# An MLP whose quarters end in a plain pair of tiles, and two first tiles that follow x together

## The chip, the cores and the metric

The kernel runs on one core of one Trainium2 chip. The core has five engines with instruction streams of their own: TensorE (PE) multiplies, VectorE (DVE) and ScalarE (ACT) do arithmetic on tiles, GpSimd (POOL) and SyncE (SP) here mostly issue DMA transfers. The engines wait for one another by semaphores. The metric is the time of one execution on the device, in microseconds; less is better.

## The reference

Two layers over 512 tokens of 1024 features. Layer 0 mixes tokens with an mLSTM (projections of x into q, k, v, an output gate and eight gate columns; a causal convolution of four taps and SiLU on q and k), layer 1 with causal pooling. Each layer then attends to 256 memory tokens and applies an MLP. After every part x becomes LayerNorm(alpha x + part(x)). The two parts that the change touches are:

```python
proj = x @ w_in                     # q, k, v, output gate, 8 gate columns
qk = silu(causal_dwconv(proj[..., :nqk], conv_w))
gates = proj[..., nqk + nv + D_MODEL:] + gate_b
...
def sq_relu_mlp(x, w1, b1, w2, b2):  # w1: 1024 x 4096, w2: 4096 x 1024
    return square(relu(x @ w1 + b1)) @ w2 + b2
```

## The kernel before

Every float32 operand of a product is split into a high part and a low part that TensorE takes at its faster float32 rate, and each product is three matmuls (`mm3`, L198 to L200): high by high, high by low, low by high. So a weight tile of 128 x 1024 comes by DMA from SP (`raw`), is cast by ScalarE (`wh`, L161) and subtracted by VectorE (`wl`, L162). `unit` does that; its first tiles take their raw space from a pool `xs`, later ones from `raw_p`.

**Front.** After a few warm-up matmuls x arrives transposed in eight K tiles (`xr`, 256 KB each), each split like the weights. The feature tile 0 of q and k (`qk0`) has weights of its own, `u0`, that come in two halves between the tiles of x. The gate weights `wgt` come ahead of K tile 2; `pg`, 16 matmuls, is the product for the gates. The scheduler of the framework puts matmuls in an order by when their operands are due, so pg's stand between qk0's while x arrives. Then come qk4 (24 matmuls), v in four token tiles (v00 to v03) and the other q and k tiles. Work that need not be done at once is deferred: `defer` and `chain` give it a time in microseconds of matmul work, and `tick`, called by each `mm3`, issues it when that time is up. The gate arithmetic (`gates`, ending in Abs, Exp and Ln on ScalarE and a scan on VectorE), its rows, its transposed `columns` and the score tiles are such work.

**MLP.** The 4096 hidden features go in four quarters q; `up_down(q)` does 0, 1 and 2. The *up phase* makes eight feature tiles of 128 in pairs m = 0, 2, 4, 6. A plain pair is two `feat_tile`s of 24 matmuls of 512 columns each, with Relu and Square by `ev` (a tile `r`, then `s`). A pair whose number stands in `STRASSEN_UP[q]` goes through `up_pair`: seven products of 12 matmuls of 256 columns into banks `ua`, `ub`, `uc`, with sums and differences of weights made by VectorE; then copies, Relu and Square into the pair's two rows of `s`. In quarter 1 the pairs 1, 2, 3 go that way and pair 0, the first, is plain; in quarter 2 all four; in quarter 0 none (its first four tiles go together).

The *down phase* is Strassen's scheme again, on blocks of 512 x 512, each block 24 matmuls of 512 columns: `u` (a11 by b11), `f` (q1 by t1), `m2` (a12 by b21), and u, u, f, u once more. In the names of tiles `h` and `l` are the high and the low part, and the two digits ahead of them are layer and quarter: q101h is the high part of q1 in layer 0, quarter 1. `q1` is the block a21 - a22 of the quarter's activations, so it needs all eight feature tiles. `t1` is a sum of two weight blocks that a DMA makes: `onto_w` (L968) lets GpSimd issue a transfer that adds the second block onto the raw tile of b11. It can go only when b11's own cast (ScalarE) and subtract (VectorE) in `weight_split` (L787, L788) have read that tile. Each block is two tiles, so two transfers. The activations are split by `split` (L778, L779).

Per engine the instructions run in program order, which the framework's scheduler settles when the kernel is built.

Of the kernel before, what the change touches and what calls it, by code (L numbers as in the profile page):

```python
# [9 lines left out]
F32 = mybir.dt.float32  # L10
# [5 lines left out]
P = 128  # L16
D = 1024
# [16 lines left out]
SUM = sum(SEG)  # L34
WU = 1024
LN_T = 7.2
STRASSEN_UP = ((), (1, 2, 3), (0, 1, 2, 3))


def f32(ap):  # L40
# [4 lines left out]
def trunk(ctx: ExitStack, tc: tile.TileContext, a: dict, out: bass.AP):  # L45
# [45 lines left out]
    def ld(dst, src):  # L91
        nc.sync.dma_start(dst, src)
# [58 lines left out]
    def unit(src):  # L151
        n = n_units[0]
        n_units[0] += 1
        if n < 5:
            r = xs_p.tile([P, D], F32, tag="xs", name=f"raw{n}")
        else:
            r = raw_p.tile([P, WU], F32, tag="raw", name=f"raw{n}")
        ld(r, src)
        h = wh_p.tile([P, WU], F32R, tag="wh", name=f"wh{n}")
        l = wl_p.tile([P, WU], F32R, tag="wl", name=f"wl{n}")  # L160
        A.copy(h, r)  # L161
        V.tensor_tensor(l, r, f32(h), ALU.subtract)  # L162
        return h, l

    def m_unit(src):
        h, l = unit(src)
        return h.rearrange("p (k m) -> p k m", m=P), l.rearrange("p (k m) -> p k m", m=P)
# [9 lines left out]
    def defer(us, fn):  # L177

        later.append([us, fn])

    def chain(us, step, fns):
        for n, fn in enumerate(fns):
            defer(us + step * n, fn)
# [13 lines left out]
    def mm3(out_, l, r, start, stop, skip=False):  # L197
        T.matmul(out_, l[0], r[0], start=start, stop=False, skip_group_check=skip)  # L198
        T.matmul(out_, l[0], r[1], start=False, stop=False, skip_group_check=skip)  # L199
        T.matmul(out_, l[1], r[0], start=False, stop=stop, skip_group_check=skip)  # L200
        if later:
            tick(3 * max(r[0].shape[-1], 128) / 2400)
# [13 lines left out]
    def hf_cols(hf):  # L216
        return slice(hf * 512, (hf + 1) * 512)
# [79 lines left out]
        for i in range(n):  # L297
            evac(i, ps[i])

    def feat_tile(name, src, x, pool_, tag, cols=slice(0, S), u=None):  # L300
        u = u or m_unit(src)
        ps = pool_.tile([P, 512], F32, tag=tag, name=name)[:, : cols.stop - cols.start]
        for k in range(KC):
            mm3(ps, (u[0][:, k], u[1][:, k]), x.k(k, cols), start=k == 0, stop=k == KC - 1)
        return ps
# [21 lines left out]
        return t  # L327

    x0 = Act("x0")
    u0 = [xs_p.tile([P, D], F32, tag="xs", name="u0r")]  # L330
    u0 += [z.tile([P, WU], F32R, tag=t, name=f"u0{t}") for z, t in ((wh_p, "wh"), (wl_p, "wl"))]

    def u0_part(z):
        r, h, l = (w[:, hf_cols(z)] for w in u0)
        ld(r, a["w_qk"][0][:, hf_cols(z)])
        A.copy(h, r)
        V.tensor_tensor(l, r, f32(h), ALU.subtract)

    wgt = None
    for q in range(4):  # L340
        if q == 1:
            wgt = gate_weights()
        r = vkv(f"xr{q}", F32)[:, : 2 * S].rearrange("p (z t) -> p z t", z=2)
        for z in range(2):
            k = 2 * q + z
            ld(r[:, z], a["xT"][:, k])
            h, l = x0.k(k)
            A.copy(h, r[:, z])
            V.tensor_tensor(l, r[:, z], f32(h), ALU.subtract)
            if k % 4 == 0:  # L350
                u0_part(k // 4)
    u0 = [w.rearrange("p (k m) -> p k m", m=P) for w in u0[1:]]

    pg = tmp_p.tile([P, 512], F32, tag="tmp", name="pg")
    for k in range(KC):
# [9 lines left out]
        return qk.k(4 * (h // 2) + h % 2), qk.k(4 * (h // 2) + 2 + h % 2)  # L365

    def conv(c):
        ps = feat_tile(f"qk{c}", a["w_qk"][c], x0, aux_p, "aux", u=u0 if c == 0 else None)
        ac = t2(f"ac{c}")
        A.activation(ac, ps, AF.Copy, scale=convw[:, c, 3:4])  # L370
        for j in range(1, 4):
            V.scalar_tensor_tensor(ac[:, j:], ps[:, : S - j], convw[:, c, 3 - j : 4 - j], ac[:, j:], ALU.mult, ALU.add)
        f = t2(f"f{c}")
        A.activation(f, ac, AF.Silu)
        h, l = qk_k(c % H)[c // H]
        if c < H:
            A.activation(h, f, AF.Copy, scale=DK ** -0.5)
            V.scalar_tensor_tensor(l, f, DK ** -0.5, f32(h), ALU.mult, ALU.subtract)
        else:
            A.copy(h, f)  # L380
            V.tensor_tensor(l, f, f32(h), ALU.subtract)
# [84 lines left out]
        A.activation(emcol.rearrange("p a b -> p (a b)"), pc[:, 16:32], AF.Exp, scale=-1.0)  # L466

    chain(5, 3.5, [gates] + [lambda s=s: gate_rows(s) for s in range(NT)])
    defer(21, columns)
    for j, c in enumerate((5, 2, 6, 3, 7, None, None, None)):  # L470
        hf, t = j // 4, j % 4
        if j == 4:
            w_v = h_units(a["w_v"][hf])
        ps = token_proj(f"v{hf}{t}", x0, w_v, t)
        for q in range(2):
            h = 2 * hf + q
            split_psum((vh[h][:, t, :256], vl[h][:, t, :256]), ps[:, q * 256 : (q + 1) * 256])
        if c is not None:
            conv(c)
        if j in (0, 2, 4):  # L480
            chain((18, 13, 10)[j // 2], 2, scores(j // 2))

    normg = const_tile("normg", [P, KC])
    b1 = const_tile("b1", [P, DEPTH, DFF // P])
# [169 lines left out]
    for i in range(DEPTH):  # L654
# [147 lines left out]
        def block(r, c):  # L802

            return xm.half(c, slice(256 * r, 256 * r + 256))

        def x_sums():
# [42 lines left out]

            chain(3, 5, [start, q3, q1, q2, q4, end])  # L850

        def up_pair(q, m, n, s):


            src = [a["w1"][i, 8 * q + m + z] for z in range(2)]
            h2 = slice(0, 512), slice(512, 1024)
            u1, u2 = [raw_p.tile([P, WU], F32, tag="raw", name=f"up{n}{m + z}") for z in range(2)]
            ld(u1, src[0])
            ld(u2, src[1])
            ta, tb = [scoped["rawd"].tile([P, WU], F32, tag="rawd", name=f"ut{n}{m}{z}") for z in "ab"]  # L860

            def hl(name, r):
                h, l = [p.tile([P, WU], F32R, tag=t, name=f"{name}{n}{m}{t}")[:, : r.shape[1]] for p, t in ((wh_p, "wh"), (wl_p, "wl"))]
                A.copy(h, r)
                V.tensor_tensor(l, r, f32(h), ALU.subtract)
                return [tuple(z[:, c].rearrange("p (k m) -> p k m", m=P) for z in (h, l)) for c in h2[: r.shape[1] // 512]]

            b11, b21 = hl("ub", u1)
            V.tensor_tensor(ta[:, h2[0]], u1[:, h2[0]], u2[:, h2[0]], ALU.add)
            V.tensor_tensor(tb[:, h2[0]], ta[:, h2[0]], u2[:, h2[1]], ALU.add)  # L870
            V.tensor_tensor(tb[:, h2[1]], tb[:, h2[0]], u1[:, h2[1]], ALU.add)
            t2_, t4 = hl("utb", tb)
            V.tensor_tensor(ta[:, h2[1]], u2[:, h2[0]], u2[:, h2[1]], ALU.add)
            t1, t3 = hl("uta", ta)
            (b22,) = hl("ud", u2[:, h2[1]])

            pa = acc_p.tile([P, 512], F32, tag="acc", name=f"ua{n}{m}")[:, :256]
            pb = acc_p.tile([P, 512], F32, tag="acc", name=f"ub{n}{m}")[:, :256]
            pc = aux_p.tile([P, 512], F32, tag="aux", name=f"uc{n}{m}")[:, :256]
            z1, z2 = s[:, m % 4], s[:, m % 4 + 1]  # L880
            lo, hi = slice(0, 256), slice(256, 512)

            def prod(ps, w, x_, start):
                for k in range(4):
                    mm3(ps, (w[0][:, k], w[1][:, k]), (x_[0][:, k], x_[1][:, k]), start=start and k == 0, stop=k == 3, skip=not start)

            prod(pa, b11, block(0, 0), True)
            A.copy(z1[:, lo], pa)
            prod(pc, b21, block(0, 1), True)
            V.tensor_tensor(z1[:, lo], z1[:, lo], pc, ALU.add)  # L890
            prod(pa, t2_, xq["q2"], False)
            A.activation(z2[:, lo], pa, AF.Copy, scale=-1.0)
            prod(pb, t1, xq["q1"], True)
            A.copy(z2[:, hi], pb)
            prod(pa, t3, xq["q3"], False)
            V.tensor_tensor(z2[:, hi], z2[:, hi], pa, ALU.subtract)
            prod(pb, b22, xq["q4"], False)
            V.tensor_tensor(z2[:, lo], z2[:, lo], pb, ALU.add)  # L898
            prod(pa, t4, block(1, 1), False)
            A.copy(z1[:, hi], pa)  # L900
            for c, z in enumerate((z1, z2)):
                A.activation(z, z, AF.Relu, bias=b1[:, i, 8 * q + m + c : 8 * q + m + c + 1], scale=1.0)  # L902
                A.activation(z, z, AF.Square)

        def up_down(q, n):

# [38 lines left out]
            for m in range(first, KC, 2):  # L945
                if m // 2 in STRASSEN_UP[q]:
                    up_pair(q, m, n, s[m // 4])
                else:
                    for z in range(2):
                        ev(m + z, feat_tile(f"h{n}{m + z}", a["w1"][i, 8 * q + m + z], xm, aux_p, "aux"))  # L950
                if m == 2:
                    first_blocks()

            def onto(row, hf, op=ALU.add):
# [150 lines left out]
```

## Time and profile before

| what | us |
|---|---|
| median of 3 runs | 1243.29 |
| lowest, highest | 1242.1, 1243.35 |
| the profiled execution, its own time | 1241.42 |
| its span in the trace | 1239.7 |
| PE busy in it | 1191.8 |
| DVE busy | 857.7 |
| ACT busy | 617.9 |
| POOL busy | 62.1 |

A span counts from the first to the last instruction; what the execution takes beyond it lies around it. Matmuls overlap in the pipeline, so a single row's duration of 0.39 us is not its price: the distance between the starts of two rows is. The mean granted TensorE clock of this execution was 0.981 of full.

### The profile page before, as it was taken

Reading aid. Unit: us, or ns where it says so; the run is one execution under the profiler, and the core shown is the slowest. Engines: PE = TensorE matmul, PEld = TensorE weight load, DVE = VectorE, ACT = ScalarE, POOL = GpSimd, SP = SyncE. Lnnn points to the kernel's source line nnn. Section 1 sums busy time; section 2 is a strip of 40 time slices with the busy share of each in tenths; the row PEclk is TensorE's granted clock in tenths of the full one; section 3 lists DMA queues with packets and bytes.
Section 4 is the critical chain, followed back from the end, with each engine's and each line's share of the span. In section 5 each row is a group of like instructions: output and inputs, shape, how many; then the busy total and the mean of one; then the engine's idle time right before and its main releaser. Section 6 shows DMA issues by size and latency. Waiting matters only on the chain.

```text
span 1239.7 us, 16808 instructions
## 1 busy us (share of the span) xinstructions
PE 1191.8 (96%) x6609; PEld 1035.7 (84%) x6609; DVE 857.7 (69%) x1191; ACT 617.9 (50%) x924; POOL 62.1 (5%) x99
## 2 busy tenths in 40 slices
PE   9999999999999999799799999999999979979997
PEld 7888898898889789689688889988988968968886
DVE  6673575575567996597585599866889659758336
ACT  6585864135324646446446443652464554644430
POOL 0221000000000100100100000000010010010000
PEclk9999999999999999899899999999999989989999
DMA  8253258433255535835745455626453482583411
GB/s 277 77 143 108 86 189 294 146 103 102 82 156 154 102 85 168 172 68 175 165 114 194 127 185 195 192 86 186 139 117 79 158 175 65 181 177 85 119 52 68
DMA packets 50976, 171.85 MB, mean 139 GB/s; under 512 B 6336, under 2 KB 6604, under 8 KB 50896
## 3 DMA queue, kind: packets, MB, share of 16 engines
q1 hardware_dynamic: 42960, 142.96, 35.8%
q0 software_dynamic: 7936, 27.81, 12.5%
q8 instruction: 52, 0.85, 0.3%
q14 instruction: 28, 0.23, 0.1%
HBM read 164.43 MB, written 6.31 MB: 138 GB/s over the span
## 4 chain that ended last, share of the span: by engine, by line
PE 79%; DVE 9%; DMA 5%; ACT 4%; issue 2%; SPq 0%; DVEq 0%; ACTq 0%
PE h L198 5%; PE h L199 5%; PE h L200 5%; PE m L199 3%; PE m L198 3%; PE m L200 3%; DMA b<-in_w 3%; PE u L198 2%; PE u L199 2%; PE u L200 2%; PE ao L198 2%; PE ao L200 2%; PE ao L199 2%; PE q L198 2%; PE q L199 2%; PE q L200 2%
## 5 line engine op out<-in xcount | busy, mean ns | idle before, releaser
L162 DVE TENSOR_TENSOR wl<-raw,wh 128x1024 fp32r<-128x1024 f32 x147 | 179.1, 1220 | 145.9 <-ACT wh L161 143.9
L161 ACT CAST wh<-raw 128x1024 fp32r<-128x1024 f32 x147 | 153.7, 1049 | 226.3 <-PE h L199 52.4
L968 POOL DMA_DIRECT2D b<-in_w x36 | 31.7, 882 | 282.4 <-DVE b1100l L788 62.7
L968 POOL DMA_DIRECT2D t<-in_w x12 | 11.5, 996 | 680.0 <-DMA t<-in_w 451.2
L249 ACT ACTIVATE rs<-mv,eps_t 128x1 f32<-128x1 f32 x24 | 7.1, 295 | 53.2 <-DVE mv L247 53.2
L198 PE MATMUL h<-xm10h,wh 128*128 128x512 f32 (+1 forms) x88 | 31.0, 352 | 0.0
L198 PE MATMUL h<-xm00h,wh 128*128 128x512 f32 (+1 forms) x88 | 31.0, 352 | 0.0
L198 PE MATMUL h<-xm01h,wh 128*128 128x512 f32 (+1 forms) x88 | 31.0, 352 | 0.0
L198 PE MATMUL h<-xm11h,wh 128*128 128x512 f32 (+1 forms) x88 | 31.0, 352 | 0.0
L199 PE MATMUL h<-xm00l,wh 128*128 128x512 f32 (+1 forms) x88 | 30.9, 352 | 0.0
L199 PE MATMUL h<-xm10l,wh 128*128 128x512 f32 (+1 forms) x88 | 30.9, 351 | 0.0
L200 PE MATMUL h<-xm00h,wl 128*128 128x512 f32 (+1 forms) x88 | 30.8, 350 | 0.0
L200 PE MATMUL h<-xm01h,wl 128*128 128x512 f32 (+1 forms) x88 | 30.8, 350 | 0.0
L200 PE MATMUL h<-xm10h,wl 128*128 128x512 f32 (+1 forms) x88 | 30.8, 350 | 0.0
L200 PE MATMUL h<-xm11h,wl 128*128 128x512 f32 (+1 forms) x88 | 30.8, 350 | 0.0
L199 PE MATMUL h<-xm01l,wh 128*128 128x512 f32 (+1 forms) x88 | 30.8, 350 | 0.0
L199 PE MATMUL h<-xm11l,wh 128*128 128x512 f32 (+1 forms) x88 | 30.8, 350 | 0.0
L677 ACT ACTIVATE pr<-s,nm 128x256 f32<-128x256 f32 x32 | 14.9, 471 | 10.4 <-DVE nm L672 7.6
L902 ACT ACTIVATE s<-s,b 128x512 f32<-128x512 f32 x28 | 18.9, 718 | 2.0 <-DVE s L898 2.0
L199 PEld LDWEIGHTS h<-xm10l,wh 128*128 128x128 f32 x88 | 16.7, 189 | 2.3
L199 PEld LDWEIGHTS h<-xm00l,wh 128*128 128x128 f32 x88 | 16.7, 189 | 2.2
L198 PEld LDWEIGHTS h<-xm00h,wh 128*128 128x128 f32 x88 | 16.7, 189 | 2.2
(1696 smaller groups left out, 4259.3 us busy)
## 6 DMA issues: line engine op xcount, KB each, us to landing
raw<-in_w SPq DMA_DIRECT2D x60, 512.0 KB, 3.8
b<-in_w SPq DMA_DIRECT2D x36, 512.0 KB, 4.5
b<-in_w POOLq DMA_DIRECT2D x36, 512.0 KB, 5.7
up<-in_w SPq DMA_DIRECT2D x28, 512.0 KB, 3.7
raw<-in_w_q SPq DMA_DIRECT2D x24, 512.0 KB, 4.1
raw<-in_w_ao SPq DMA_DIRECT2D x16, 512.0 KB, 3.7
t<-in_w SPq DMA_DIRECT2D x12, 512.0 KB, 3.8
t<-in_w POOLq DMA_DIRECT2D x12, 512.0 KB, 9.8
```

The source lines that it names most:

```text
L161: A.copy(h, r)
L162: V.tensor_tensor(l, r, f32(h), ALU.subtract)
L198: T.matmul(out_, l[0], r[0], start=start, stop=False, skip_group_check=skip)
L199: T.matmul(out_, l[0], r[1], start=False, stop=False, skip_group_check=skip)
L200: T.matmul(out_, l[1], r[0], start=False, stop=stop, skip_group_check=skip)
L249: A.activation(rs, mv[:, 1:2], AF.Sqrt, bias=eps_t, scale=1.0)
L677: A.activation(pr[:, ms], ps[:, ms], AF.Exp, bias=nm[:, t_ : t_ + 1], scale=1.0, accum_out=sm[:, t_ : t_ + 1])
L902: A.activation(z, z, AF.Relu, bias=b1[:, i, 8 * q + m + c : 8 * q + m + c + 1], scale=1.0)
L968: G.dma_start(z[w], a["w2"][i, q, hf, j + w], accum_op=ALU.add)
```

## The change

Three things. In the MLP `STRASSEN_UP` names the pairs 0, 1, 2 in both quarters 1 and 2: in quarter 1 the plain pair moves from the first place to the last, in quarter 2 the fourth pair becomes plain. The seventh product of a Strassen pair, with the copies, Relu and Square of both its rows, is kept in `open_pairs` and issued by `last_product` behind the first product of the next pair, and for the last pair behind the first plain tile. `first_blocks`, the preparation of a11's blocks, stands at the third pair.

At the front the feature tiles 0 and 4 go through the K tiles of x together, each in a bank of its own, with weights in three pieces (K tiles 0 and 1, 2 and 3, 4 to 7); the gate weights come ahead of K tile 4; pg comes behind all of x. Gate columns and the first scores are deferred by 3 us more.

```diff
-STRASSEN_UP = ((), (1, 2, 3), (0, 1, 2, 3))
+STRASSEN_UP = ((), (0, 1, 2), (0, 1, 2))
...
-    def u0_part(z):
-        r, h, l = (w[:, hf_cols(z)] for w in u0)
-        ld(r, a["w_qk"][0][:, hf_cols(z)])
+    first = {}
+    for c in (0, 4):
+        first[c] = [xs_p.tile([P, D], F32, tag="xs", name=f"u{c}r")]
+        first[c] += [z.tile([P, WU], F32R, tag=t, name=f"u{c}{t}") for z, t in ((wh_p, "wh"), (wl_p, "wl"))]
+        first[c].append(aux_p.tile([P, 512], F32, tag="aux", name=f"qk{c}"))
+
+    def first_part(c, k0, k1):
+        r, h, l = (w[:, k0 * P : k1 * P] for w in first[c][:3])
+        ld(r, a["w_qk"][c][:, k0 * P : k1 * P])
         A.copy(h, r)
         V.tensor_tensor(l, r, f32(h), ALU.subtract)
 
     wgt = None
+    first_part(0, 0, 2)
     for q in range(4):
-        if q == 1:
+        if q == 2:
             wgt = gate_weights()
...
-            if k % 4 == 0:
-                u0_part(k // 4)
-    u0 = [w.rearrange("p (k m) -> p k m", m=P) for w in u0[1:]]
+            for c, n, k0, k1 in ((4, 0, 0, 2), (0, 1, 2, 4), (4, 2, 2, 4), (0, 3, 4, 8), (4, 4, 4, 8)):
+                if n == k:
+                    first_part(c, k0, k1)
+            for c in (0, 4):
+                _, wh, wl, ps = first[c]
+                mm3(ps, (wh[:, tok(k)], wl[:, tok(k)]), x0.k(k), start=k == 0, stop=k == KC - 1)
...
-    defer(21, columns)
+    defer(24, columns)
...
-            chain((18, 13, 10)[j // 2], 2, scores(j // 2))
+            chain((21, 13, 10)[j // 2], 2, scores(j // 2))
...
+        open_pairs = []
+
+        def last_product():
+
+            while open_pairs:
+                open_pairs.pop()()
+
         def up_pair(q, m, n, s):
...
             A.copy(z1[:, lo], pa)
+            last_product()
             prod(pc, b21, block(0, 1), True)
...
-            prod(pa, t4, block(1, 1), False)
-            A.copy(z1[:, hi], pa)
-            for c, z in enumerate((z1, z2)):
-                A.activation(z, z, AF.Relu, bias=b1[:, i, 8 * q + m + c : 8 * q + m + c + 1], scale=1.0)
-                A.activation(z, z, AF.Square)
+
+            def last():
+                prod(pa, t4, block(1, 1), False)
+                A.copy(z1[:, hi], pa)
+                for c, z in enumerate((z1, z2)):
+                    A.activation(z, z, AF.Relu, bias=b1[:, i, 8 * q + m + c : 8 * q + m + c + 1], scale=1.0)
+                    A.activation(z, z, AF.Square)
+
+            open_pairs.append(last)
...
                     for z in range(2):
                         ev(m + z, feat_tile(f"h{n}{m + z}", a["w1"][i, 8 * q + m + z], xm, aux_p, "aux"))
-                if m == 2:
+                        last_product()
+                if m == 4 and first == 0:
                     first_blocks()
```

In program order this is what moves. On ScalarE, before, from the first cast t101h of layer 0, quarter 1, to q101h (s011 are the rows of the second four feature tiles):

```order
L787 CAST t101h0_4723<-b11010_4682 128x1024
L787 CAST t101h1_4727<-b11011_4683 128x1024
L900 COPY s011_4226<-ua016_4578 128x256
L902 ACTIVATE s011_4226<-s011_4226,b1_985 128x512
L902 ACTIVATE s011_4226<-s011_4226,b1_985 128x512
L903 ACTIVATE s011_4226<-s011_4226 128x512 x2
L787 CAST b2101h0_4771<-b21010_4763 128x1024
L787 CAST b2101h1_4775<-b21011_4764 128x1024
L778 CAST q101h_4733<-s010_4225 128x1024
```

The same place now:

```order
L794 CAST t101h0_4732<-b11010_4691 128x1024
L934 ACTIVATE r016_4631<-h016_4606,b1_994 128x512
L794 CAST t101h1_4736<-b11011_4692 128x1024
L935 ACTIVATE s011_4235<-r016_4631 128x512
L917 COPY s011_4235<-ua014_4493 128x256
L919 ACTIVATE s011_4235<-s011_4235,b1_994 128x512
L920 ACTIVATE s011_4235<-s011_4235 128x512
L794 CAST b2101h0_4780<-b21010_4772 128x1024
L934 ACTIVATE r017_4682<-h017_4657,b1_994 128x512
L935 ACTIVATE s011_4235<-r017_4682 128x512
L785 CAST q101h_4742<-s010_4234 128x1024
```

The rows of the last Strassen pair (016 before, 014 now) stand between t101h and b2101h as before, and the Relu and Square of the plain tiles h016 and h017 stand ahead of q101h.

On GpSimd, before, the accumulating transfers of the same quarter's down phase:

```order
L968 DMA t3010_4805<-in_w2 128x1024
L968 DMA b11010_4682<-in_w2 128x1024
L968 DMA t3011_4806<-in_w2 128x1024
L968 DMA b11011_4683<-in_w2 128x1024
L968 DMA b11010_4682<-in_w2 128x1024
L968 DMA b11011_4683<-in_w2 128x1024
```

And now:

```order
L988 DMA t3010_4814<-in_w2 128x1024
L988 DMA t3011_4815<-in_w2 128x1024
L988 DMA b11010_4691<-in_w2 128x1024
L988 DMA b11011_4692<-in_w2 128x1024
L988 DMA b11010_4691<-in_w2 128x1024
L988 DMA b11011_4692<-in_w2 128x1024
```

Both transfers for t3 have moved ahead of the first one for t1 (the first row of b11010).

On VectorE at the front, before, from the gates' scan L452 to the weight subtract wl8 (the weights of qk2):

```order
L452 SCALAR_TENSOR_TENSOR gb_348<-ga_347 4x512
L455 SCALAR_TENSOR_TENSOR bc_349<-ga_347 4x512
L208 TENSOR_TENSOR vl1_192<-v00_353,vh1_188 128x256
L456 TENSOR_TENSOR gb_348<-ga_347,bc_349 4x128
L378 SCALAR_TENSOR_TENSOR qk0l_237<-f1_316,qk0h_236 128x512
L457 TENSOR_TENSOR bc_349<-bc_349,gb_348 4x512
L455 SCALAR_TENSOR_TENSOR bc_349<-ga_347 4x384
L455 SCALAR_TENSOR_TENSOR bc_349<-ga_347 4x256
L456 TENSOR_TENSOR gb_348<-ga_347,bc_349 4x128 x2
L457 TENSOR_TENSOR bc_349<-bc_349,gb_348 4x384
L162 TENSOR_TENSOR wl8_472<-raw8_469,wh8_471 128x1024
```

Now, up to the same weights' subtract, here wl7:

```order
L459 SCALAR_TENSOR_TENSOR gb_357<-ga_356 4x512
L208 TENSOR_TENSOR vl1_257<-v00_362,vh1_253 128x256
L462 SCALAR_TENSOR_TENSOR bc_358<-ga_356 4x512
L379 SCALAR_TENSOR_TENSOR ac5_436<-qk5_407,convw_250,ac5_436 128x511
L463 TENSOR_TENSOR gb_357<-ga_356,bc_358 4x128
L379 SCALAR_TENSOR_TENSOR ac5_436<-qk5_407,convw_250,ac5_436 128x510
L464 TENSOR_TENSOR bc_358<-bc_358,gb_357 4x512
L379 SCALAR_TENSOR_TENSOR ac5_436<-qk5_407,convw_250,ac5_436 128x509
L462 SCALAR_TENSOR_TENSOR bc_358<-ga_356 4x384
L208 TENSOR_TENSOR vl0_256<-v01_445,vh0_252 128x256
L463 TENSOR_TENSOR gb_357<-ga_356,bc_358 4x128
L162 TENSOR_TENSOR wl7_481<-raw7_478,wh7_480 128x1024
```

The weights of qk2 stand behind the gates' scan in both, now with the convolution of qk5 between them. PE's own order in the four transitions is now: the last pair's other products, h016, the pair's seventh product (ua014), h017, u, f. At the front it is: qk0 and qk4 in turns for each K tile, pg, then v00 and qk1; 116 matmuls stand between the first of v00 and the first of qk2 that needs wl.

## Rows read from the trace of the kernel before

**Rows 1.** The page, parts 1 and 2: busy times, granted clock in slices.

```profile
PE 1191.8 (96%) x6609; PEld 1035.7 (84%) x6609; DVE 857.7 (69%) x1191; ACT 617.9 (50%) x924; POOL 62.1 (5%) x99
PEclk9999999999999999899899999999999989989999
```

**Rows 2.** Waits of PE: engine, line, for whom: us in total, times, longest.

```profile
PE f L198 <- ACT q111h L778: 8.5, 1, 8.5
...
PE f L198 <- ACT q101h L778: 7.9, 1, 7.9
PE ua L198 <- DVE s L896: 1.9, 4, 0.8
```

**Rows 3.** PE's timeline (start us, us, instruction, idle before), first and last long wait.

```profile
511.06 0.39 PE L199 MATMUL u<-b1101l,a1101h 128*128 128x512 f32 x1
511.29 0.39 PE L200 MATMUL u<-b1101h,a1101l 128*128 128x512 f32 x1
...
519.53 0.80 PE L198 MATMUL f<-t101h,q101h 128*128 128x512 f32 x1 [7.86 <-ACT q101h L778]
...
527.33 0.39 PE L198 MATMUL m<-b2101h,a1201h 128*128 128x512 f32 x1
...
1109.21 0.79 PE L198 MATMUL f<-t112h,q112h 128*128 128x512 f32 x1 [8.08 <-ACT q112h L778]
...
1117.41 0.39 PE L198 MATMUL m<-b2112h,a1212h 128*128 128x512 f32 x1
```

**Rows 4.** Windows: us, busy per engine, then PEclk, DMA share, GB/s.

```profile
420.00:440.00 20.00, 18.76 (x82) 14.87 (x81) 19.97 (x20) 12.81 (x15) 2.06 (x3) 1.00 0.45 93
...
512.00:514.00 2.00, 0.00 (x0) 0.00 (x0) 0.00 (x0) 0.93 (x1) 0.31 (x1) 1.00 0.67 72
...
516.00:524.00 8.00, 4.46 (x11) 3.51 (x12) 7.31 (x7) 5.38 (x7) 0.67 (x1) 0.50 0.78 159
```

**Rows 5.** ScalarE's timeline, the second cast t101h and q101h.

```profile
513.07 1.04 ACT L787 CAST t101h<-b 128x1024 fp32r<-128x1024 f32 x1 [3.30 <-DMA b<-in_w]
...
518.44 1.04 ACT L778 CAST q101h<-s 128x1024 fp32r<-128x1024 f32 x1
```

**Rows 6.** GpSimd's timeline; then DMA issues of 498:499.5, 504:506 and 404:425, us to landing last.

```profile
499.10 0.90 POOL L968 DMA_DIRECT2D b<-in_w  x1 [0.76 <-DVE b1101l L788]
...
505.15 0.88 POOL L968 DMA_DIRECT2D b<-in_w  x1 [4.24 <-DVE s L896]
...
b<-in_w POOLq DMA_DIRECT2D x1, 512.0 KB, 9.5
...
b<-in_w POOLq DMA_DIRECT2D x1, 512.0 KB, 7.8
...
b<-in_w POOLq DMA_DIRECT2D x4, 512.0 KB, 5.5
```

**Rows 7.** PE's timeline, the same place in quarter 0 of layer 0.

```profile
429.63 0.39 PE L200 MATMUL u<-b1100h,a1100l 128*128 128x512 f32 x1
430.75 0.50 PE L198 MATMUL f<-t100h,q100h 128*128 128x512 f32 x1 [0.72 <-ACT q100h L778]
...
437.15 0.39 PE L198 MATMUL m<-b2100h,a1200h 128*128 128x512 f32 x1
```

**Rows 8.** PE's timeline, matmuls of 256 columns in a Strassen pair.

```profile
505.54 0.28 PE L199 MATMUL ua<-xm01l,utb016wh 128*128 128x256 f32 x1
505.66 0.28 PE L200 MATMUL ua<-xm01h,utb016wl 128*128 128x256 f32 x1
```

**Rows 9.** Timelines at the front: PE, ScalarE, VectorE.

```profile
5.32 0.55 PE L198 MATMUL qk<-x00h,u0wh 128*128 128x512 f32 x1
...
21.62 0.39 PE L198 MATMUL v<-wh,x00h 128*128 128x512 f32 x1
...
28.19 0.63 ACT L447 ACTIVATE ga<-gb 4x512 f32<-4x512 f32 x1 [2.33 <-DVE gb L446]
...
42.92 1.21 DVE L162 TENSOR_TENSOR wl<-raw,wh 128x1024 fp32r<-128x1024 f32 x1
```

More of the change, by code (lines that the diff above doesn't have):

```diff
@@ L153, in unit @@
         n_units[0] += 1
-        if n < 5:
+        if n < 4:
             r = xs_p.tile([P, D], F32, tag="xs", name=f"raw{n}")
@@ L298, in feat_first, with feat_tile @@
             evac(i, ps[i])
-    def feat_tile(name, src, x, pool_, tag, cols=slice(0, S), u=None):
-        u = u or m_unit(src)
+    def feat_tile(name, src, x, pool_, tag, cols=slice(0, S)):
+        u = m_unit(src)
         ps = pool_.tile([P, 512], F32, tag=tag, name=name)[:, : cols.stop - cols.start]
@@ L329, in trunk @@
     x0 = Act("x0")
-    u0 = [xs_p.tile([P, D], F32, tag="xs", name="u0r")]
-    u0 += [z.tile([P, WU], F32R, tag=t, name=f"u0{t}") for z, t in ((wh_p, "wh"), (wl_p, "wl"))]
-    def u0_part(z):
-        r, h, l = (w[:, hf_cols(z)] for w in u0)
-        ld(r, a["w_qk"][0][:, hf_cols(z)])
+    first = {}
[6 more added lines that the diff above has]
+        ld(r, a["w_qk"][c][:, k0 * P : k1 * P])
         A.copy(h, r)
@@ L367, in conv @@
     def conv(c):
-        ps = feat_tile(f"qk{c}", a["w_qk"][c], x0, aux_p, "aux", u=u0 if c == 0 else None)
+        ps = first[c][3] if c in first else feat_tile(f"qk{c}", a["w_qk"][c], x0, aux_p, "aux")
         ac = t2(f"ac{c}")
```

## The prediction

> **What bounds the kernel now.** I read the page's busy table first: TensorE (PE) is busy 96% of the span, VectorE 69%, and the granted clock is under nine tenths in four of the forty slices only [rows 1]. So time can be won only by fewer matmul cycles, by closing PE's waits, or by keeping its clock. The waits of PE come next: four waits for ScalarE's cast q1h, 7.9 to 8.5 us each, in the quarters 1 and 2 of both layers, and four short ones of pairs for VectorE, 1.9 us together, stand ahead of all others [rows 2]. The slow slices are where the four long waits are.
>
> One of them in detail, layer 0, quarter 1. The block u is over at 511.29 + 0.23 = 511.52. The block f, 24 matmuls of 512 columns, is next in PE's order; it starts at 519.53 and the block m at 527.33 [rows 3]. At the pitch between u's last two rows, 0.23 (0.2267 over a whole block), f would take 5.44 us. So f costs 527.33 - 511.52 - 5.44 = 10.4 us too much: 8.0 of waiting, and 2.4 because it then runs slowly. The windows say why: while PE stands, the granted clock is still 1.00, and then it is 0.50 for about 8 us, the 1.2 GHz level, though PE has work again [rows 4]. The last of the four loses 8.08 + (1117.41 - 1109.21 - 5.44) = 10.8 [rows 3]; reckoned in the same way the two others give 10.9 and 10.7. All four: 42.8 us.
>
> What f waits for. ScalarE's second cast t101h waits for a DMA until 513.07, and q101h, behind nine rows on ScalarE, ends at 519.5 [rows 5]. That DMA is the second of the accumulating transfers that GpSimd issues onto the raw weights b11. It was issued at 505.15, landing 7.8 us later; the first, of 499.10, took 9.5 [rows 6]. They were late because b11's casts stood behind the last Strassen pair, and GpSimd had issued two transfers t beside them. So the stall is a question of order: the quarter ends in a Strassen pair of 84 x 0.12 = 10.1 us of short matmuls [rows 8], behind which u (5.44) alone covers the chain to f. Quarter 0 of the same trace is the counter-example. It ends in plain feature tiles; its four such transfers take 5.5 us [rows 6], and from u's end (429.63 + 0.23) to m at 437.15 f takes 7.29, only 1.85 too much [rows 7].
>
> **The change, part by part.** *Order of quarters 1 and 2.* Both now end in a plain pair of tiles, h016 and h017, with the last pair's seventh product between them. Call T0 the start of h016. Until f PE has 5.44 (h016) + 12 x 0.12 (product) + 5.44 (h017) + 5.44 (u) = 17.8 us of work. b11's casts on ScalarE find their slots free at T0, when the pair's other products are over; with the subtracts behind them (1.21 each, as the row of VectorE in [rows 9]) the two transfers leave at about T0+2.7 and T0+3.9. GpSimd's transfers t now stand ahead of both and are down by T0+0.5, so these have the queue to themselves. Their landing is the unknown: 5.5 us in quarter 0, 7.8 and 9.5 in the crowded case [rows 6]. I take 6.5, nearer to quarter 0, since the weights of u and of the plain tiles are in by then; the second is down at T0+10.4. From there to f, ScalarE has t1h, the Square of h016, the pair's deferred copy, Relu and Square, b21h, h017's Relu and Square and q1h: 7.7 us, against 519.5 - 513.07 = 6.4 for the like list in [rows 5]. f can start at T0+18.1, some 0.35 late, and VectorE's q1l adds another half to one us: quarter 0's figure again. So each transition keeps 1.85 and 4 x 1.85 = 7.4 of the 42.8 stay; 35.4 go. In quarter 0's transition the clock stayed at 1.00 [rows 4], so I add no slow stretch.
>
> By the Trainium skill (DMA: Bandwidth & Descriptors, Anatomy of one DMA — SWDGE (gpsimd) path), a GpSimd transfer takes 2.0 us plus its bytes over 436 GB/s, an estimate of 3.2 us for these 512 KB; the second would be down at T0+7.1, only q1l's half would be left, and the sum would come out about 1.4 us lower. None of the rows bears that out: 5.5 is the least here [rows 6], and I stay with it.
>
> *One Strassen pair less.* Quarter 2 does all four pairs by Strassen, now three. A pair of 84 short matmuls (10.08) becomes 48 long ones (10.88): +0.80 in each layer, **+1.6**. Quarter 1 only reorders.
>
> *The seventh product, deferred.* It stands behind the next pair's first product, so the fill of a pair has cover where PE waits for VectorE: 1.9 us [rows 2], which I take as gone, **-1.9**. The pairs' fills also run with gaps too small for the list of waits; from pair to pair I read 5.6 us over the ideal in all, so the gain could be 5.6; with z1's bank held longer it could be nil.
>
> *The front.* Now tiles 0 and 4 both follow x, six matmuls for each K tile, and the 16 of pg come last. PE's 64 matmuls are the same, from 5.32 to 21.62 before, 16.3 us for 14.5 of work [rows 9]. x's last tile, at the rate of the loads before, lands at about 13 with the weight pieces among them; the last six of qk and pg end at about 19.8: 1.8 us earlier. But the gates start later than that. In the trace of before, from the gates' Abs on ScalarE (28.19) through three table loads, VectorE's scans and the weight subtract wl behind them (42.92, done 44.13) go 15.9 us, and PE was about to wait for it [rows 9]. Let E be v00's start. The gate's sum now stands on VectorE behind two rows of qk1's convolution, whose matmuls end at E+6.4; ScalarE's cast, table load and scaling ahead of those rows take the sum to about E+11.7, worked out with the durations of before. So the chain starts at E+12.5 and wl, the low half of qk2's weights, is done at E+28.4. Ahead of that matmul PE has 116 x 0.2267 = 26.3 us. So PE waits 2 us there, and about 0.3 more later behind the scores. Against the 1.8 won: **+0.5**, between -1.8 (the wait hidden) and +4. Columns and scores are put back by 3 us of PE's time each; they add nothing on PE, and what they free is what their rows would wait for.
>
> **Sum**, in the profiled execution's time of 1241.4: 1241.4 - 35.4 + 1.6 - 1.9 + 0.5 = 1206.2. That execution lies 1.9 under the median of the runs, 1243.3, so **1208 us**, 2.8% less.
>
> **The rivals.** *A: the transfers stay slow.* If they take 9.5 us, as the first in [rows 6], the second is down at T0+13.4, 3.0 us later: 12 over four transitions, 1220; if the clock falls with it, f loses 2.4 more each time, 1230. For it: VectorE has a list of subtracts just then. Against it: in quarter 0 VectorE was busy for 19.97 us of 20 [rows 4], and 5.5 us it was. The Trainium skill (SBUF — State Buffer, SBUF: two separate sides) says that some VectorE instructions lock GpSimd out while it writes a transfer's descriptors; by that rule A would hold, and quarter 0's transfers speak against it.
>
> *B: no stall is left.* If they land in 5.5 us or less and q1l is in time, f starts on time: 1208 - 7.4 = 1200.6. VectorE's rows in quarter 0 speak against it, the free GpSimd queue for it.
>
> *C: slower.* The chain from the last landing to f is not shorter, and h017's rows now stand ahead of q1h on ScalarE. If the second transfer lands 14 us or more after its issue (17.8 of cover and 8.0 of wait, less 7.7 of chain and the issue at T0+3.9), the four stalls stay whole; then +1.6 of matmuls and the front's +4 give 1243.3 + 5.6 = 1249. No row of the trace shows such a landing for b.
>
> *D: the front.* If qk2's wait becomes 5 us or so, since the chain of three table loads is on the path, and PE's clock drops there as in [rows 4], the front costs 5: 1212.5.
>
> *E: the change does not do what it says.* PE's order does show h016, the deferred product, h017, u, f in all four places, so only the times are open.
>
> **How the numbers follow.** Forecast (1203 to 1213) 0.55, A 0.16, B 0.16, D 0.08, C 0.04, E 0.01. The range goes from B with half of the fills' gain, 1199, to A with a little of the front, 1223: C and the tails of A stay out. A measurement of this kernel can tell about 0.2% from no change. Only C and E do not give a clear gain: faster 0.95, same 0.01, slower 0.04.
>
> **What would show it.** PE's list of waits: q1h at under 1.5 us in four places instead of 8; the clock full in the two slices before 527 and the others of [rows 4]; PE busy 97 to 98%; the second accumulating transfer landing 5 to 7 us after issue; m 7.3 us behind u's end. At the front v00 at 19.8 and one wait of about 2 us for wl at qk2. The forecast is wrong if q1h's waits are over 4 us, if another wait takes their place (t1h, q1l, the plain tiles' wl), or if the front's wait is over 5.

## The result and the profile after

The changed kernel takes 1213.3 us in the median of 4 runs (1211.2 to 1216.7), the kernel before 1242.7 beside it. The ratio is 0.977, with a 95% interval of 0.974 to 0.980. Forecast was 1208 within 1199 to 1223. The size came out about right; why it is not 1198, as it could have been, is what the experiments found. The profiled execution took 1211.2, the least of the four.

The page of after, its busy line and the granted clock in the 40 slices; they answer to [rows 1]:

```profile
PE 1185.5 (98%) x6537; PEld 1028.7 (85%) x6537; DVE 846.9 (70%) x1176; ACT 615.7 (51%) x914; POOL 61.0 (5%) x99
PEclk9999999999999999999999999999999999999999
```

No slice is under nine tenths any more. The waits of PE in after (engine, line, for whom: us in total, times, longest), beside [rows 2]:

```profile
PE f L198 <- ACT q112h L785: 2.6, 1, 2.6
PE f L198 <- ACT q101h L785: 2.2, 1, 2.2
PE qk L200 <- DVE wl L162: 2.0, 1, 2.0
...
PE f L198 <- ACT q111h L785: 0.9, 1, 0.9
...
PE f L198 <- ACT q102h L785: 0.6, 1, 0.6
PE ua L198 <- ACT s L907: 0.6, 1, 0.6
```

The four waits of 7.9 to 8.5 us are down to 2.2, 0.6, 0.9 and 2.6, and the new wait for `wl` at the front is there. PE's timeline at the end of u in layer 0, quarter 1, the place of [rows 3]:

```profile
513.78 0.39 PE L200 MATMUL u<-b1101h,a1101l 128*128 128x512 f32 x1
516.41 0.50 PE L198 MATMUL f<-t101h,q101h 128*128 128x512 f32 x1 [2.24 <-ACT q101h L785]
...
524.25 0.39 PE L198 MATMUL m<-b2101h,a1201h 128*128 128x512 f32 x1
```

Reckoned as in the prediction, f costs 524.25 - 514.01 - 5.44 = 4.8 us too much: 2.4 ahead of it and 2.4 in it. The windows of after there and in layer 1, quarter 2 (us, busy time of PE, PEld, DVE, ACT, POOL, then PEclk, DMA share, GB/s) show the slow part:

```profile
514.00:516.00 2.00, 0.17 (x1) 0.00 (x0) 1.97 (x4) 0.71 (x2) 0.00 (x0) 1.00 1.02 203
516.00:522.00 6.00, 5.00 (x15) 3.73 (x16) 5.01 (x5) 4.15 (x5) 0.00 (x0) 0.72 0.27 95
...
1080.00:1086.00 6.00, 5.41 (x17) 3.98 (x16) 4.77 (x7) 3.21 (x4) 0.00 (x0) 0.72 0.22 58
```

A wait of 2.2 or 2.6 us was followed by some 3.4 us at half clock in either place; the waits of 0.6 and 0.9 were not, and f lost 1.8 and 2.1 there. The four losses are 4.8, 1.8, 2.1 and 5.2: 13.9 us, where they were 42.8 (43.0 if the last one, 11.0, is reckoned from u's end like the others). The two places that the clock left at full speed lost 1.0 in f, by the wait for q1l above all, so the half clock's own part of the 2.4 is some 1.4 us.

Where the time went, by the starts of PE's blocks in the two traces. Up to u of layer 0, quarter 0 (which holds the front) after is 2.2 us behind (426.64 against 424.42). The four losses at f give back 29.1 (43.0 less 13.9). The up phases of quarters 1 and 2, from the end of the last down phase to the end of u, give back 3.1 with the 1.6 for the missing Strassen pair in it (47.5, 46.6, 46.6 and 46.6 us now; 47.2, 48.2, 47.3 and 47.7 before). Everything between differs by less than 0.1. Together 30.0; the last matmul starts 30.05 earlier (1201.38 against 1231.43).

### The profile page after: what moved, and what is told of

The parts are those of the page before. It is cut to its first block, busy times and chain, and to the rows that moved or that the text cites. A ratio compares the mean times of both kernels' runs of the same rounds, so it can differ in the third digit from the quotient of the medians.

```text
span 1209.4 us, 16635 instructions
## 1 busy us (share of the span) xinstructions
PE 1185.5 (98%) x6537; PEld 1028.7 (85%) x6537; DVE 846.9 (70%) x1176; ACT 615.7 (51%) x914; POOL 61.0 (5%) x99
## 4 chain that ended last, share of the span: by engine, by line
PE 80%; DVE 8%; DMA 5%; issue 3%; ACT 3%; POOL 1%; SPq 0%; DVEq 0%; POOLq 0%; ACTq 0%
PE h L199 4%; PE h L198 4%; PE h L200 4%; PE m L200 3%; PE m L198 3%; PE m L199 3%; DMA b<-in_w 3%; PE u L199 3%; PE u L198 3%; PE u L200 3%; PE ao L198 2%; PE ao L199 2%; PE ao L200 2%; PE q L198 2%; PE q L199 2%
## 5 line engine op out<-in xcount | busy, mean ns | idle before, releaser
L162 DVE TENSOR_TENSOR wl<-raw,wh 128x1024 fp32r<-128x1024 f32 x150 | 182.9, 1221 | 152.2 <-ACT wh L161 150.4
L161 ACT CAST wh<-raw 128x1024 fp32r<-128x1024 f32 x150 | 157.1, 1049 | 226.4 <-PE h L199 51.7
L988 POOL DMA_DIRECT2D t<-in_w x12 | 10.7, 916 | 646.0 <-DMA t<-in_w 408.3
L198 PE MATMUL h<-xm10h,wh 128*128 128x512 f32 (+1 forms) x96 | 34.2, 356 | 0.0
L198 PE MATMUL h<-xm00h,wh 128*128 128x512 f32 (+1 forms) x96 | 34.2, 356 | 0.0
L199 PE MATMUL h<-xm00l,wh 128*128 128x512 f32 (+1 forms) x96 | 34.1, 355 | 0.0
L199 PE MATMUL h<-xm10l,wh 128*128 128x512 f32 (+1 forms) x96 | 34.1, 355 | 0.0
L200 PEld LDWEIGHTS h<-xm10h,wl 128*128 128x128 f32 x96 | 18.2, 189 | 2.6
L198 PEld LDWEIGHTS h<-xm01h,wh 128*128 128x128 f32 x96 | 18.2, 189 | 2.5
L198 PEld LDWEIGHTS h<-xm11h,wh 128*128 128x128 f32 x96 | 18.2, 189 | 2.5
L199 PEld LDWEIGHTS h<-xm01l,wh 128*128 128x128 f32 x96 | 18.2, 189 | 2.5
```

The lines of the kernel that those rows point to most:

```text
L988: G.dma_start(z[w], a["w2"][i, q, hf, j + w], accum_op=ALU.add)
```

## The experiments

Theory at the start: the new order of pairs does all of the work at f, the deferral fills gaps in the pairs, the front costs 2 us. The rival: it is the deferred product behind h016 that keeps PE fed.

**The order of pairs alone.** The kernel before with two edits, the old front, nothing deferred.

```diff
-STRASSEN_UP = ((), (1, 2, 3), (0, 1, 2, 3))
+STRASSEN_UP = ((), (0, 1, 2), (0, 1, 2))
...
-                if m == 2:
+                if m == 4 and first == 0:
                     first_blocks()
```

> The kernel before with only the order of pairs changed: quarters 1 and 2 do the pairs 0, 1, 2 by Strassen and end in the plain pair; no product is deferred, the front is the old one. My theory (PE's cover between the accumulating transfers and f is what counts): the four waits of f for q1h fall from about 8 us to between 0.6 and 3 us, so some 27 to 33 us go, the pairs' gaps (some 5 us) stay, the one Strassen pair less costs 1.6: 1211 to 1217 us. Rival (the deferred seventh product behind h016 is what keeps f fed): two tiles alone leave waits of 5 us or more and the half clock, 1225 to 1240 us.

Measured: 1198.4 us (1197.7 to 1199.2), ratio 0.966 (0.964 to 0.967). That is 15 us less than after, and 13 less than the low end that I expected. The waits of PE in it, all of 0.3 us and more:

```profile
PE warm L312 <- POOL zero L309: 1.3, 1, 1.3
PE po L200 <- DVE d1l L208: 1.1, 1, 1.1
PE f L198 <- ACT q110h L778: 0.7, 1, 0.7
PE f L198 <- ACT q100h L778: 0.7, 1, 0.7
PE f L200 <- DVE q112l L779: 0.6, 1, 0.6
PE f L200 <- DVE q110l L779: 0.5, 1, 0.5
PE f L200 <- DVE q100l L779: 0.5, 1, 0.5
PE f L198 <- ACT q112h L778: 0.3, 1, 0.3
```

Of the four places in quarters 1 and 2 only the last still waits for q1h, 0.3 us; f loses 0.2, 0.2, 0.3 and 1.4 us at the four. Its up phases take 47.2, 46.8, 47.1 and 46.8 us. So the order does the work at f, and nearly all of the pairs' gain too: the deferral improves the up phases by 0.5 us in all. By this reckoning it costs some 12 us at f (13.9 against 2.2); a run below tests that.

**The deferral alone.** Old pairs and old front; `up_pair` and `last_product` as in the change, a11's blocks one pair later, and the last pair's product at the end of the loop over m:

```diff
+            open_pairs.append(last)
...
-                if m == 2:
+                        last_product()
+                if m == 4 and first == 0:
                     first_blocks()
+            last_product()
```

> The kernel before with only the seventh products deferred (old pairs, old front; the last pair's one is done right behind its other products, and a11's blocks are prepared one pair later). My theory: the four waits for q1h stay at about 8 us with the half clock behind them; only the pairs' gaps shrink, by 3 to 5 us over the two layers: 1238 to 1240 us. Rival (the deferral makes the gain): waits under 4 us, 1220 us or less.

Measured: 1236.5 us (1233.2 to 1240.1), ratio 0.996 (0.995 to 0.998). The waits for q1h are 10.2, 9.5, 7.3 and 6.7 us: they stay, and the rival falls for the old order. The gain, 4.6 us by the medians, is that of the pairs' gaps: the four up phases take 185.8 us in its trace, 190.4 before.

**The front alone.** The kernel before with the new front.

> The kernel before with only the new front (tiles 0 and 4 together through x, three pieces of weights, gates later). My theory from the trace of after: v starts at the same 21.6 us as before, since x's third tile lands 1.4 us later behind the smaller pieces, and PE waits 2 us at qk2 for wl behind the gates' scans: 1.5 to 2.5 us slower than before, 1244 to 1245.5 us. Rival, as the prediction had it: v starts 1.8 us earlier, +0.5 us net, 1243 us.

Measured: 1243.2 us (1242.3 to 1247.4), ratio 1.0024 (1.0011 to 1.0037): +3 us, between 1.4 and 4.6. The traces bear the size out: up to u of layer 0, quarter 0, where the kernels differ in the front alone, the five with the old front take 424.4 to 425.4 us (424.7 in the mean) and the seven with the new one 426.6 to 428.8 (427.6), 2.9 us more; after's 2.2 is the least of them. The wait at qk2 is 2.0 us in all seven; where the rest is lost was not placed. The time at which v starts, and the wait at qk2, PE's timeline of after:

```profile
21.60 0.39 PE L198 MATMUL v<-wh,x00h 128*128 128x512 f32 x1
...
50.20 0.50 PE L200 MATMUL qk<-x00h,wl 128*128 128x512 f32 x1 [2.00 <-DVE wl L162]
```

v starts where it started before (21.62, [rows 9]), and the 2.0 us at qk2 come on top. ScalarE's timeline shows why nothing was won by then. The casts of x's third K tile, first before, then after:

```profile
6.80 0.62 ACT L348 CAST x00h<-xr 128x512 fp32r<-128x512 f32 x1 [0.59 <-DMA xr<-in_xT]
```

```profile
8.22 0.62 ACT L352 CAST x00h<-xr 128x512 fp32r<-128x512 f32 x1 [1.37 <-DMA xr<-in_xT]
```

In the first six microseconds SP issues a transfer every 0.47 us, of 128 KB or of 256, in both. With the 128 KB pieces between them the third tile's transfer leaves at 3.08 and its cast waits until 8.22, where it left at 2.59 and was cast at 6.80: 0.5 us of the delay is the later issue, the rest a longer way. The window from 6 to 8 us, before and after, shows that the DMA engines moved less:

```profile
6.00:8.00 2.00, 2.00 (x9) 1.37 (x9) 1.52 (x3) 0.87 (x3) 0.11 (x1) 1.00 1.02 289
```

```profile
6.00:8.00 2.00, 1.98 (x9) 1.35 (x8) 1.03 (x2) 0.84 (x2) 0.10 (x1) 1.00 0.65 188
```

What made the rate fall is not shown. SP's pace does not explain it: between 2.13 and 4.03 it issued 768 KB, some 414 GB/s, and the window moved 188.

**After with the old front.** The edit is the reverse of the change's front, with the deferral times of columns and scores.

> The kernel after with the front of before (new order of pairs and deferral kept). My theory: 2 us faster than after, 1210 to 1212 us, no wait at qk2 of more than 0.3 us. Rival (the front is neutral): 1213 us. Which of the four waits for q1h are 2 us or more (in after: layer 0 quarter 1 and layer 1 quarter 2) may change, if it is instruction loads that make one of the accumulating transfers land late there, since the program's rows shift against them.

Measured: 1207.4 us (1203.3 to 1209.4), ratio 0.972 (0.970 to 0.975): 6 us less than after by the medians and under the 1210 that I expected at the least, though the two intervals just overlap; about 3 of the 6 are the front. In its trace, of its slowest execution, f still loses 5.1, 1.8, 4.6 and 2.7 us. The waits of 2.3 and 1.9 us for q1h there were followed by a granted clock of 0.73 and 0.72 over six microseconds, those of 1.5 and 0.6 by 1.00. So the places where it is worst are not fixed; another trace of the same order of work gives another set. I had thought of instruction transfers that fall into one accumulating transfer; of the places with a late landing some have one in their window and some don't, so that stays open. Nor do the bytes that SP's transfers moved beside them go with the landing times over the places read.

**After without the deferral.**

```diff
-            open_pairs.append(last)
+            last()
```

> The kernel after with the deferral undone alone (the seventh product and its copies, Relu and Square stand behind the pair's other products again; new order of pairs, new front). My theory, formed after the first four runs (the deferral costs f time: it puts 1.7 us of ScalarE rows into the chain from the last accumulating transfer to q1h and sends the first such transfer 0.6 us later against u): f's four waits fall under 1 us, the time is the order-only kernel's plus 2 us of front, 1199 to 1202 us. Rival (the good result of the order-only kernel came from the old front or from its luck with landing times): 1208 us or more.

Measured: 1200.9 us (1199.9 to 1202.2), ratio 0.967 (0.966 to 0.968). One line is worth 12 us by the medians. f loses 0.2, 0.9, 0.3 and 0.2, together 12.3 less than in after. The rival, luck of the first kernel, falls. (The spans of the two profiled executions are only 9.0 apart: this one, the slowest of its four, lost 3.2 more at the front, in the up phases and between the layers.)

How the deferral delays f can be seen in the two traces. First VectorE in the order-only kernel, then in after, up to the two subtracts of b11:

```profile
492.32 1.22 DVE L939 TENSOR_TENSOR s<-s 128x1024 f32<-128x1024 f32 x1
493.46 0.41 DVE L896 TENSOR_TENSOR s<-s,ua 128x256 f32<-128x256 f32 x1
493.79 1.22 DVE L788 TENSOR_TENSOR b1101l<-b,b1101h 128x1024 fp32r<-128x1024 f32 x1
...
496.39 1.22 DVE L788 TENSOR_TENSOR b1101l<-b,b1101h 128x1024 fp32r<-128x1024 f32 x1
```

```profile
493.86 1.23 DVE L786 TENSOR_TENSOR a1101l<-s,a1101h 128x1024 fp32r<-128x1024 f32 x1 [0.51 <-ACT a1101h L785]
495.03 0.42 DVE L911 TENSOR_TENSOR s<-s,ua 128x256 f32<-128x256 f32 x1
495.37 1.22 DVE L958 TENSOR_TENSOR s<-s 128x1024 f32<-128x1024 f32 x1
496.50 0.41 DVE L913 TENSOR_TENSOR s<-s,ub 128x256 f32<-128x256 f32 x1
496.83 2.35 DVE L795 TENSOR_TENSOR b1101l<-b,b1101h 128x1024 fp32r<-128x1024 f32 x2
```

In after a11's split and its difference (L958) are late, since the second pair's rows are finished only behind the third pair's first product, and b1101l stands behind them. Then GpSimd's accumulating transfers, the order-only kernel first, each with its DMA rows (us to landing last):

```profile
495.41 0.89 POOL L968 DMA_DIRECT2D b<-in_w  x1 [4.80 <-DMA up<-in_w]
498.01 0.87 POOL L968 DMA_DIRECT2D b<-in_w  x1 [1.72 <-DVE b1101l L788]
...
b<-in_w POOLq DMA_DIRECT2D x1, 512.0 KB, 5.5
...
b<-in_w POOLq DMA_DIRECT2D x1, 512.0 KB, 5.8
```

```profile
498.45 0.89 POOL L988 DMA_DIRECT2D b<-in_w  x1 [5.53 <-DMA up<-in_w]
499.59 0.87 POOL L988 DMA_DIRECT2D b<-in_w  x1 [0.25 <-issue]
...
b<-in_w POOLq DMA_DIRECT2D x1, 512.0 KB, 7.5
...
b<-in_w POOLq DMA_DIRECT2D x1, 512.0 KB, 8.9
```

For the first transfer the rows name the DMA of `up` as releaser; but it leaves 0.40 us behind the end of the first subtract b1101l in the order-only kernel, as the second does behind the second subtract in both (0.40 and 0.41), so I take the subtract for it in after too. u starts at 506.14 and 508.56, so the first transfer leaves 10.7 us ahead of u there, and 10.1 here. The two transfers are closer together here, but that costs nothing by itself: over the 28 places of the seven kernels with the new order and f in its old place, the second lands 9.1 us behind the first one's issue in the mean, both for the 16 places with 2.6 us between the two issues and for the 12 with 1.1. The two fill the DMA engines by themselves: from 498.45 to 506.45 in after GpSimd's queue took 88% of the 16 engines' time, SP's loads 12%. The rest is ScalarE. Its timeline in after from the second t101h, which starts as its transfer is down (499.59 + 8.9 = 508.49), to q101h:

```profile
508.57 1.05 ACT L794 CAST t101h<-b 128x1024 fp32r<-128x1024 f32 x1 [0.90 <-PE h L199]
509.52 0.63 ACT L935 ACTIVATE s<-r 128x512 f32<-128x512 f32 x1
510.05 0.35 ACT L917 COPY s<-ua 128x256 f32<-128x256 f32 x1
510.44 0.72 ACT L919 ACTIVATE s<-s,b 128x512 f32<-128x512 f32 x1
511.19 0.63 ACT L920 ACTIVATE s<-s 128x512 f32<-128x512 f32 x1
511.73 1.03 ACT L794 CAST b2101h<-b 128x1024 fp32r<-128x1024 f32 x1
...
515.31 1.04 ACT L785 CAST q101h<-s 128x1024 fp32r<-128x1024 f32 x1 [1.29 <-DVE s L994]
```

The copy and L919 and L920 are the last pair's deferred rows, 1.7 us, and q1 needs them all: from landing to f go 7.9 us in all four places. In the order-only kernel, at its one place where f waits for q1h, it is 6.2 (the transfer lands at 1061.26, f starts at 1067.45), without those rows:

```profile
1061.29 1.05 ACT L787 CAST t112h<-b 128x1024 fp32r<-128x1024 f32 x1 [1.97 <-DMA b<-in_w]
1062.24 0.63 ACT L916 ACTIVATE s<-r 128x512 f32<-128x512 f32 x1
1062.77 1.03 ACT L787 CAST b2112h<-b 128x1024 fp32r<-128x1024 f32 x1
...
1066.35 1.05 ACT L778 CAST q112h<-s 128x1024 fp32r<-128x1024 f32 x1 [1.29 <-DVE s L974]
```

So from the first issue PE has 10.7 + 5.4 = 16.1 us of work without the deferral, and the chain takes 9.1 + 6.2 = 15.3 at the mean landing: 0.8 to spare. With it there are 10.1 + 5.4 = 15.5 against 9.1 + 7.9 = 17.0: 1.5 too late, before any late landing. That is an estimate from these rows.

**Two halves of the deferral.** To tell the two delays apart: the deferral for the first pair only, for all but the last pair, and for the last pair only. The test in front of `open_pairs.append(last)` is `m > 0`, `m == 4` and `m < 4`; where it holds, `last()` runs at once.

> The kernel after in which only the last pair of a quarter (m = 4) does its seventh product at once; between pairs it is deferred as in after. My theory: the harm sits in the last pair alone, so this has the time of the kernel without deferral or 0.5 to 1 us less (the pairs' gaps): 1198.5 to 1202 us. Rival (the deferral between pairs costs something too): 1205 us or more.

> The kernel after with the deferral kept for the first pair of a quarter only (m = 0); the pairs m = 2 and m = 4 do their seventh product at once. My theory: deferring pair m = 2 makes the row 3 of the activations late, and with it the difference a11 - a21, behind which VectorE's subtract b11l stands; that subtract lets the first accumulating transfer go. With pair 2 undeferred that transfer leaves 10.7 us ahead of u's start, as in the kernel without deferral, not 10.1: f's waits under 1 us, 1199.5 to 1202.5 us. Rival (any deferral between pairs costs what the variant with the last pair undeferred showed): 1204 us or more.

> The kernel after with the deferral kept for the last pair alone (m = 4, its seventh product behind the tile h016). My theory: the first accumulating transfer leaves 10.7 us ahead of u, as without deferral, but ScalarE has the deferred copy, Relu and Square (1.7 us) between the casts t1h and q1h, so f can start some 7.9 us after the second landing instead of 6.2 to 6.9: f loses 0.2 to 2.5 us at each of the four places, 1202 to 1208 us, between the kernel without deferral (1201) and after (1213). Rival (only the transfer's issue counts, not ScalarE's list): 1199.5 to 1201.5 us.

| deferred | us (lowest, highest) | ratio (95% interval) | f loses at the four places |
|---|---|---|---|
| none | 1200.9 (1199.9, 1202.2) | 0.967 (0.966, 0.968) | 0.2, 0.9, 0.3, 0.2 |
| pair m = 0 | 1199.7 (1199.3, 1204.1) | 0.967 (0.965, 0.969) | 0.4, 0.3, 0.6, 1.4 |
| pairs m = 0, 2 | 1205.3 (1202.9, 1206.3) | 0.970 (0.968, 0.972) | 2.0, 0.6, 0.8, 0.7 |
| pair m = 4 | 1205.0 (1200.8, 1206.6) | 0.970 (0.967, 0.972) | 0.4, 1.3, 1.2, 0.4 |
| all (after) | 1213.3 (1211.2, 1216.7) | 0.977 (0.974, 0.980) | 4.8, 1.8, 2.1, 5.2 |

The expectation for the kernel with pairs 0 and 2 deferred, the first of the three to run, failed: I had put all harm into the last pair. Its trace showed the first transfer leaving 10.1 us ahead of u at all four places, as in after; that led to the next run, where only pair 0 is deferred: 10.7 there, and no harm. The last pair alone costs 4 us too by the medians, though its interval overlaps that of none. Landing to f was not the 7.9 us that I expected there: where f waited it took 7.0, since part of the deferred rows ran ahead of the second landing. With pairs 0 and 2 it took 6.9 where f waited, the Relu of h016 standing behind the second cast there. In the reckoning above the cover is then 0.5 us short with pairs 0 and 2, and just used up with pair 4. So either half costs about 4 us and both 12: together the small delays are over the cover, and then the clock falls at two places. Not all of the 4 us of each half is in f's losses of its one trace (2.6 and 1.7 more than with none). In the trace with pairs 0 and 2, 2.5 us more stand between layer 0's last down phase and layer 1's first, in rows that the edit does not touch; for pair 4 the rest is not placed.

**More cover instead.** The block m2 ahead of f, in after and in the order-only kernel. It needs neither q1 nor t1, so 5.4 us more of PE's work stand ahead of f.

```diff
+            b21 = load("b21", 0, 2)
+            l12 = split(f"a12{n}", a12)
+            product(m2, l12, weight_split(f"b21{n}", b21), True, onto(0, 0))
             V.tensor_tensor(a21, a21, a22, ALU.subtract)
             w = weight_split(f"t1{n}", b)
             onto_w(b, 1, 2)
             product(f, split(f"q1{n}", a21), w, True, onto(1, 1))
-            b21 = load("b21", 0, 2)
-            l12 = split(f"a12{n}", a12)
-            product(m2, l12, weight_split(f"b21{n}", b21), True, onto(0, 0))
```

> The kernel after with the block m2 (a12 by b21) ahead of f in the down phase of quarters 0 to 2; deferral and new front kept. 5.4 us more of PE's work stand between u and f. My theory (f's lateness is only a matter of cover for the chain behind the accumulating transfers): all six waits ahead of f vanish, with the slow clock behind two of them, so 13.9 us in quarters 1 and 2 and 3.6 in quarters 0 go: 1194 to 1199 us. Rival (q1h or another resource waits for u's end or for PE, so the wait moves along with f): 1207 us or more.

> The order-only kernel (old front, no deferral) with m2 ahead of f. My theory: the 1.85 us in each of the two quarters 0 and the 2.2 us that the other four still lose go: 1198.4 - 5.9 = 1192 to 1194 us, the best of all. Rival (m2's operands b21 and a12 come too late in their new place and m2 waits instead): 1198 us or more.

Measured: 1202.9 us (1201.9 to 1204.3), ratio 0.969 (0.967 to 0.970), from after's 1213.3; but 1202.3 us (1201.8 to 1202.9), ratio 0.968 (0.967 to 0.970), from the order-only kernel's 1198.4. In both the waits for q1h are gone from quarters 1 and 2, so f's lateness was a matter of cover. Both sums were wrong, though: 1194 to 1199 and 1192 to 1194 were expected, and in the two quarters 0 f still loses 1.5 us or so of its 1.8. PE's waits in the second of them, the longest three:

```profile
PE u L198 <- DVE xp L957: 2.2, 2, 1.1
PE ua L198 <- DVE s L896: 1.9, 2, 1.3
PE u L198 <- DVE xin L957: 1.7, 2, 0.9
```

VectorE now reaches the drain of u's bank (L957) later than PE needs the bank for the next u, and the following up phase in quarter 2 is 1.0 to 1.5 us longer than in the order-only kernel; the down phases of quarters 1 and 2 come out about 1 us longer, but for the last. Where f had hardly waited, the waits that take its place are larger.

**The best kernel run** is the order of pairs alone: 1198.4 us, 0.966 (0.964 to 0.967) of before. The one with pair 0 deferred and the new front, 0.967 (0.965 to 0.969), is not told apart from it; that deferral with the old front was not run.

## Why the prediction was right, and where its steps failed

**What bounds the kernel: right.** The four waits and the half clock behind them were the time to win. Of the three parts only the order of pairs touches their cause for the better, and that edit alone brings 42.7 us.

**The four transitions: the mechanism right, the term mis-sized.** 7.4 us were to stay, 13.9 did. The issue and the chain hold: the second transfer left at T0 + 3.4 (predicted 3.9; T0 is 496.20 in layer 0, quarter 1), and landing to f took 7.9 (predicted 7.7). The landing failed: 6.5 was taken, 8.9, 7.3, 7.5 and 9.3 were measured. Two of the four lie near the end that rival A used, 9.5; those places lost 3.0 and 3.4 us more than forecast: 1.5 and 1.9 by the longer wait and 1.4 by the clock, where A had 3.0 and 2.4. So "I add no slow stretch" held for two places and not for the two others. I had reasoned from quarter 0, where the transfers go singly, 5 to 7 us apart; here two go within 1.1 us and share the DMA engines, and both were down only 8.4 to 10.4 us after the first issue. Two readings were slightly off without harm: the last loss is 11.0 from u's end, not 10.8, and seven rows, not nine, stand between t101h and q101h in [rows 5].

The estimate of 3.2 us for such a transfer from the fit in the Trainium skill (DMA: Bandwidth & Descriptors, Anatomy of one DMA — SWDGE (gpsimd) path) differs from every row: none of the accumulating transfers for b in the twelve traces landed in less than 5.0 us, alone or not. The measurement decides. Whether the adding makes the difference no run shows, since every transfer of that size from GpSimd adds.

**The deferred product: wrong.** It was booked as -1.9, up to -5.6, from the pairs' fills. The fills did shrink by 4.7 us, near the upper end, but the new order does that too: the deferral adds 0.5. The step that failed is that the deferral was priced by PE's gaps alone; its cost in the list of ScalarE's rows between the last landing and f was not set against it. I wrote the deferred copy, Relu and Square into it, found 7.7 us, and compared that with before, not with the same order without deferral. Nor did I ask who waits for the second pair's rows: a11's blocks, and behind them on VectorE b11's subtract. Undoing one line is worth 12 us; the traces show for it 0.6 us less of lead for the first transfer and 1.7 us more of ScalarE's rows at each of four places, and the half clock at two.

**The front: half right.** The 2 us at qk2 came: with E at 21.60, wl was predicted for E + 28.4 = 50.0, and the matmul starts at 50.20. The 1.8 us ahead of it did not come: I had x's transfers arrive at the old rate with the pieces between them, but the rate fell in the window from 6 to 8 us. +0.5 was forecast, +2.2 is in after's trace, +2.9 between the means of the traces and +3 in the runs.

**The Strassen pair less:** the 0.8 us in each layer are not seen apart, since the quarter 2 that loses the pair also loses its gaps; its up phase is 1.1 to 1.6 us shorter all the same.

**The sum** was nearly right in part by luck: 6.5 us too little at f and 1.7 too little at the front stood against 2.8 too little for the pairs, and the 12 us that the deferral cost at f were small beside the 40 that the order of pairs won there. The time alone would not have shown that one of the three parts costs 12 us. Of the rivals, A came half true; C, a slower kernel, had its point at a landing of 14 us, which nothing came near.

## What to carry to other kernels

A change of several parts that comes out faster may hide a part that costs: the order of pairs alone beats the whole change by 15 us, and the one-line reversal of the deferral showed it. Work deferred to fill one engine's gap still stands in the lists of the others; follow each deferred row to whoever needs its result (here q1 on ScalarE, and a11's blocks, with the DMA behind them) before it is booked as free. A chain with slack of a us or two is best costed with its worst measured landing, since a wait that is long enough costs more when the clock falls behind it (here 1.4 us on top of 2.4).

## What the runs showed of the hardware

Two accumulating transfers of 512 KB from GpSimd, issued 1.1 or 2.6 us apart, are down 9.1 us after the first issue in the mean (8.1 to 10.4 over 28 places); in the two kernels with m2 ahead of f, where the loads of b21 are issued beside them, it was 8.6 to 12.8. One alone, as the first four of each quarter 0, took 5.0 to 6.7. Waits of PE of 1.9, 2.2, 2.3 and 2.6 us for q1h (old front and after) were followed by some 3.4 us at half clock; waits of 0.6, 0.9 and 1.5 us, with another 0.6 for q1l four matmuls later, were not. In the front the DMA engines' share fell from 1.02 to 0.65 in the window from 6 to 8 us when 128 KB pieces stood between the tiles of x; why is not shown.
